# Second block of a two-block network: k, v, q and the Fourier input token major from float32r parts, rotation on the free axis, Fourier over half the tokens

## The chip, the core and the metric

The kernel runs on one core of one Trainium2 chip. A time is device microseconds of one execution; the time of a kernel is the median of several runs.

## What is computed

The reference chains two transformer blocks over 256 tokens of width 1024. The first block (projections, sparse attention, a convolution, a mixture of 64 experts) is not touched by the change. The second block has two layers; the change is in the mixer of its first layer, cut here to what matters:

```python
xn   = modulate(rms_norm_2(h, norm_mix_g), sh1, sc1)      # 256 x 1024
proj = xn @ w_in                                          # Fourier 512, q 512, k 128, v 128
q, k = apply_rope(q, cos, sin), apply_rope(k, cos, sin)   # pairs (2j, 2j+1) of each 64 wide head
attn = window_attention(q, k, v, k_ctx, v_ctx, sink)      # 8 heads, 2 kv heads, 256 + 256 keys
y    = concat([fourier_mix(f_in), attn]) @ w_out
h    = h + g1 * y                                         # then norm, SwiGLU (the first FFN)

def fourier_mix(u):                                       # per head of 128 columns
    return fftn(u, axes=(token, column), norm='ortho').real
```

## The kernel before

The weights stream from HBM through a ring of six slots of 2 MB (`wslot`); SyncE's queue issues the loads in program order, each when its slot is free. In the mixer the slots hold, in order, the k and v columns (`kv2`), q, the Fourier columns (`f`), the two halves of `ada2_2`, the two halves of the output weights (`out2`), `ada2_3`, `ada2_4`, and then the first loads of the FFN, among which are further `ada` matrices.

`even` builds the normalized input (`norm_mod`) feature major, eight tiles of 128 features by 256 tokens, and then weaves four generators: `attention2`, `gemvs2`, `projections`, `second_out`. A model of the engines (`_Model`) decides at build time in which order their instructions are written, and under `manual_schedule` the order so written is the order in which TensorE, VectorE and ScalarE run them. Each engine works its list from the top; nothing behind a waiting instruction starts.

- `projections` computes one 128 column tile after the other (k, q0, v, q1, q2, q3, then four Fourier heads) with float32 matmuls of 256 columns. After k and each q tile, `rope` copies the tile, multiplies it on TensorE by a swap matrix, and combines the two with cosine and sine on VectorE.
- `attention2` works on eight units (four head pairs by two blocks of 128 queries). `scores2` makes a unit's 128x512 scores for two heads and its softmax: VectorE adds the mask and takes the maximum (a custom instruction, printed as CUSTOM_DVE or ISA), ScalarE the exponentials, VectorE and GpSimd scale. `attend2` transposes the probabilities on TensorE, ScalarE copies them (`p2T`), TensorE multiplies with the values. Scores of the next unit are written ahead of the transposes of the present one.
- `dft` makes one Fourier head: two matmuls with the 128 point matrix, a copy (`fz`), four matmuls with the 256 point matrices.
- `gemvs2` makes three gate and scale vectors of the layer on VectorE: eight multiply-adds of 128x1024 each (`acc`), then a sum and a transpose on TensorE. It starts with the event `q1`.
- `second_out` is the output projection: eight tiles of eight matmuls. The first three tiles take the three PSUM banks called `g`; a further tile needs a bank that VectorE has emptied by adding it to `x`.

In the FFN that follows, the weights are used as two float32r parts already: `split2` rounds on ScalarE (`whi`), takes the difference on VectorE or GpSimd (`wlo`), and three matmuls take the place of one. The scheduler, not the written order, places the FFN's first instructions among those of the mixer.

## Time and profile before

| | |
|---|---|
| median of 3 runs | 1718.29 us (1717.68 to 1720.73) |
| profiled execution | 1721.32 us, of which the span of the trace is 1719.5 us |
| busy share of the span | TensorE 79%, VectorE 33%, ScalarE 22%, GpSimd 8% |
| granted TensorE clock, mean | 0.887 |
| DMA | 589.51 MB, mean 343 GB/s |

Shares of the whole span are an average over stages. Until about 1155 us the experts stream their weights and the DMA engines are full; the mixer of the second block lies between about 1164 and 1286 us; after it come the two FFNs with the pooling mixer between them. Times in the text are microseconds from the start of the span.

### The profile page before, as it was taken

To read this page: it belongs to the slowest core of one execution; us is meant where nothing else is said; L and a number is where in the kernel's file an instruction comes from. 1 tells how busy PE (TensorE), PEld (TensorE's weight loads), DVE (VectorE), ACT (ScalarE), POOL (GpSimd) and SP (SyncE) were. 2 spreads that over 40 slices of the span, in tenths; PEclk is the share of its full clock that TensorE was granted. 3 is DMA by queue.
4 is the path that set the end of the run, shared out by engine and by line. 5 is a ranking of instruction groups with operands and counts; after the bars stand their busy time and mean duration, and the time that the engine had idled before them with its cause. 6 is when DMAs were issued, how large, how long until landed. Compare 5 with 4: busy or idle time off the path is not lost.

```text
span 1719.5 us, 18422 instructions
## 1 busy us (share of the span) xinstructions
PE 1361.6 (79%) x7664; PEld 788.7 (46%) x7664; DVE 575.8 (33%) x1109; ACT 375.6 (22%) x704; POOL 143.0 (8%) x80
## 2 busy tenths in 40 slices
PE   7999976666765765666576676769989999999997
PEld 5676832221221221222122212216667778778886
DVE  1577721110110111111011101105575878454533
ACT  2335110000000000100000000013324444554444
POOL 0000000000000000000000000001202232213224
PEclk9999988878887787788788778889999999999999
DMA  9687889999999999899999999997476786635620
GB/s 402 244 342 300 317 370 427 427 426 426 427 428 427 427 426 425 340 427 426 426 426 427 428 427 427 426 426 285 184 298 243 301 340 260 245 147 220 245 74 25
DMA packets 43563, 589.51 MB, mean 343 GB/s; under 512 B 4840, under 2 KB 4968, under 8 KB 6992
## 3 DMA queue, kind: packets, MB, share of 16 engines
q1 hardware_dynamic: 42336, 584.82, 82.2%
q0 software_dynamic: 704, 2.64, 0.4%
q8 instruction: 63, 1.03, 0.2%
q10 hardware_dynamic: 432, 0.79, 0.1%
q14 instruction: 28, 0.23, 0.0%
HBM read 587.16 MB, written 1.06 MB: 342 GB/s over the span
## 4 chain that ended last, share of the span: by engine, by line
PE 31%; DMA 24%; DVE 3%; ACT 1%; issue 0%; DVEq 0%; ACTq 0%
PE ps L264 31%; DMA w<-in_w 22%; DMA w<-in_w2last 1%; DVE acc L264 1%; DMA w<-in_ada 0%; DVE wlo L264 0%; DVE p L264 0%; ACT p L264 0%; DVE x L264 0%; ACT rstd L264 0%; DVE ada L264 0%; DVE sqa L264 0%; DVE mix L264 0%; ACT mix L264 0%; ACT sq L264 0%
## 5 line engine op out<-in xcount | busy, mean ns | idle before, releaser
L264 PE MATMUL ps<-w,xg 128*32 128x512 f32 x2032 | 304.3, 735 | 178.1 <-DMA w<-in_w 177.9
L264 PE MATMUL ps<-w,gT 128*32 128x512 f32 x1024 | 180.7, 843 | 100.3 <-DMA w<-in_w 91.3
L264 PEld LDWEIGHTS ps<-w,xg 128*32 128x32 f32 x2032 | 64.9, 123 | 397.2 <-DMA w<-in_w 208.0
L264 ACT ACTIVATE whi<-w 128x1024 fp32r<-128x1024 f32 x132 | 139.4, 1059 | 152.1 <-PE ps L264 146.5
L264 DVE TENSOR_TENSOR g<-g,ps 128x512 f32<-128x512 f32 x16 | 11.0, 687 | 451.1 <-PE ps L264 451.1
L264 DVE TENSOR_TENSOR wlo<-w,whi 128x1024 fp32r<-128x1024 f32 x88 | 114.6, 1310 | 111.5 <-ACT whi L264 111.5
L264 PE MATMUL ps<-whi,mix 128*128 128x512 f32 x352 | 140.4, 404 | 4.1 <-ACT mix L264 4.1
L264 DVE SCALAR_TENSOR_TENSOR acc<-w,sil,acc 128x1024 f32<-128x1024 f32 x98 | 141.8, 1447 | 2.7 <-DMA w<-in_ada 1.1
L264 POOL TENSOR_TENSOR wlo<-w,whi 128x1024 fp32r<-128x1024 f32 x44 | 112.6, 2569 | 350.2 <-ACT whi L264 293.2
L264 PE MATMUL ps<-wlo,mix 128*128 128x512 f32 x352 | 140.5, 400 | 0.0
L264 PE MATMUL ps<-whi,xl 128*128 128x512 f32 x352 | 138.6, 399 | 0.9 <-DVE xl L264 0.9
L264 PEld LDWEIGHTS ps<-w,gT 128*32 128x32 f32 x1024 | 33.6, 134 | 229.0 <-DMA w<-in_w 147.4
L264 DVE COPY y<-ps 128x512 f32<-128x512 f32 x16 | 11.1, 691 | 282.1 <-PE ps L264 282.1
L264 ACT ACTIVATE gT<-ps 128x512 f32<-128x512 f32 x16 | 9.6, 597 | 320.6 <-PE ps L264 320.6
L264 PE MATMUL ps<-hT,w 128*128 128x256 f32 x320 | 77.4, 389 | 2.4 <-DVE hT L264 2.4
L264 PEld LDWEIGHTS ps<-whi,mix 128*128 128x128 f32 x352 | 67.5, 192 | 22.2 <-ACT mix L264 5.3
L264 DVE SCALAR_TENSOR_TENSOR x<-ps,mod,x 128x256 f32<-128x256 f32 x152 | 67.3, 482 | 28.8 <-PE ps L264 28.6
L264 PE MATMUL ps<-oh,xtok 128*128 128x128 f32 x512 | 62.9, 284 | 16.4 <-DVE oh L264 16.4
L264 PEld LDWEIGHTS ps<-whi,xl 128*128 128x128 f32 x352 | 67.3, 191 | 16.6 <-DVE xl L264 1.7
L264 PEld LDWEIGHTS ps<-wlo,mix 128*128 128x128 f32 x352 | 67.6, 192 | 14.6 <-DVE wlo L264 0.4
L264 PEld LDWEIGHTS ps<-oh,xtok 128*128 128x128 f32 x512 | 61.8, 200 | 18.1 <-DVE oh L264 16.5
L264 PE MATMUL ps<-wlo,gh 128*128 128x512 f32 x176 | 69.7, 399 | 0.0
(302 smaller groups left out, 1511.5 us busy)
## 6 DMA issues: line engine op xcount, KB each, us to landing
w<-in_w SPq DMA_DIRECT2D x190, 2048.0 KB, 26.1
w<-in_ada SPq DMA_DIRECT2D x34, 2048.0 KB, 10.2
w<-in_f SPq DMA_DIRECT2D x32, 2048.0 KB, 8.4
w<-in_wout SPq DMA_DIRECT2D x4, 2048.0 KB, 9.3
w<-in_win SPq DMA_DIRECT2D x3, 2048.0 KB, 23.7
w<-in_conv SPq DMA_DIRECT2D x4, 1536.0 KB, 11.8
w<-in_ada1h SPq DMA_DIRECT2D x2, 2048.0 KB, 13.4
w<-in_cw SPq DMA_DIRECT2D x2, 2048.0 KB, 12.0
```

The costliest lines, as they stand in the source:

```text
L264: r = f(*args, **kw)
```

## The change

The diff, with the constant tables, the packing and some removed lines left out:

```diff
         self.ring = pool("ring", RING)
+        self.xtra = pool("xtra", 4)
...
-    def rope(self, out, ps, scale, name):
...
+    def half(self, w, c):
+        src = w[:, D * c:D * c + D]
+        hi, lo = [self.xtra.tile([P, D], F32R, tag="x", name=self.nm(n)) for n in ("whi", "wlo")]
+        nc.scalar.activation(hi, src, AF.Copy)
+        for eng, s in ((nc.vector, slice(0, 512)), (nc.gpsimd, slice(512, D))):
+            eng.tensor_tensor(lo[:, s], src[:, s], hi[:, s].bitcast(F32), ALU.subtract)
+        return hi, lo
...
+    def tm_gemm(self, ps, chunks, cols):
+        m = D // cols
+        for c in chunks:
+            yield from self.ahead_half(c + 1)
+            ws = self.halves[c]
+            for kk in range(m):
+                k = m * (c - chunks[0]) + kk
+                yield self.ready(ws[1][:, cols * kk:cols * kk + cols], self.hl[:, k, :])
+                for t in range(2):
+                    st = slice(P * t, P * t + P)
+                    hi, lo = [x[:, cols * kk:cols * kk + cols] for x in ws]
+                    self.mm(ps[t][:, :cols], lhsT=self.hh[:, k, st], rhs=hi, start=k == 0, stop=False)
+                    self.mm(ps[t][:, :cols], lhsT=self.hh[:, k, st], rhs=lo, start=False, stop=False)
+                    self.mm(ps[t][:, :cols], lhsT=self.hl[:, k, st], rhs=hi, start=False, stop=k == KT - 1)
+                yield self.clock
+            yield from self.ahead_half(c + 2)
+    def rope(self, src, t, scale):
+        q = self.wk(512, "ada")[:, :n]
+        nc.scalar.activation(q, src, AF.Copy, scale=scale)
...
+        nc.vector.tensor_tensor(pairs(r), pairs(q)[:, :, :, ::-1], sin[:, None].to_broadcast([P, n // 64, 32, 2]), ALU.mult)
...
+        nc.vector.tensor_tensor(qh, qh, cos[:, None].to_broadcast([P, n // 64, 64]), ALU.mult)
+        nc.vector.tensor_tensor(q, q, r, ALU.add)
+        return q
+    def fourier(self, i, f):
         pz = self.ps()
         for t in range(2):
+            self.mm(pz[:, :S], lhsT=f[:, t, P * i:P * i + P], rhs=self.late("dft")[:, S * t:S * t + S],
+                    start=t == 0, stop=t == 1)
+        z = self.ph(S, "fz", 2)
+        nc.scalar.activation(z, pz[:, :S], AF.Copy)
...
+        self.mm(po[:, :129], lhsT=cs[:, :P], rhs=z[:, :129], start=True, stop=True)
+        self.mm(po[:, S:S + 127], lhsT=cs[:, P:], rhs=z[:, 129:], start=True, stop=True)
+        q = self.ph(127, "fq", 2)
+        nc.scalar.activation(q, po[:, S:S + 127], AF.Copy)
+        nc.vector.tensor_copy(o[:, ::P], po[:, :S:P])
+        nc.vector.tensor_tensor(o[:, 1:P], po[:, 1:P], q, ALU.subtract)
+        nc.vector.tensor_tensor(o[:, P + 1:], po[:, P - 1:0:-1], q[:, ::-1], ALU.add)
...
     def projections(self):
+        ps = yield from self.grab("g", 2)
+        yield from self.tm_gemm(ps, (0, 1), S)
+        for t in range(2):
+            nc.vector.tensor_copy(self.vall[:, 0, t, :], ps[t][:, P:S])
+            k.append(self.rope(ps[t][:, :P], t, 1.0))
...
+        yield from self.tm_gemm(ps, (2, 3, 4, 5), 512)
+        q = [self.rope(ps[t], t, 0.125) for t in range(2)]
...
+        self.spawn(self.turned(q, [self.qT[:, :, P * t:P * t + P] for t in range(2)], [f"q{i}" for i in range(4)]))
...
+        yield from self.tm_gemm(ps, (6, 7, 8, 9), 512)
...
+            nc.scalar.activation(f[:, t, :], ps[t], AF.Copy)
...
+    def turned(self, src, outs, names):
...
+                self.tr(pt[:, P * i:P * i + P], x[:, P * i:P * i + P])
+            self.nc.vector.tensor_copy(o, pt[:, :P * n].rearrange("p (i s) -> p i s", i=n))
...
+        self.parts = [("kv2", i) for i in range(2)] + [("q", i) for i in range(4)] + [("f", i) for i in range(4)]
+        self.halves = [self.half(self.ahead[n][0][1], i) for n, i in self.parts[:2]]
+        h = self.hh = self.ph(0, "h", shape=[P, KT, S], dt=F32R)
+        self.hl = self.ph(0, "hl", shape=[P, KT, S], dt=F32R)
...
+        nc.gpsimd.dma_start(self.mask[:, 0, P:2 * P], a["wm"][0])
...
+        self.norm_mod(self.x, self.scaled(self.v2("norm_mix_g_2", 0), self.m2(0, 1)), self.m2(0, 0),
+                      parts=(h, self.hl))
```

The normalized input is now kept as two float32r parts (`hh`, `hl`), and the weights are split in ten pieces of 128x1024 (`half`; two for k and v, four for q, four for the Fourier columns), of which two are in flight. Tokens stand on the output's partitions: k and v are one pass of eight steps of 256 columns, q and the Fourier input one pass each of eight steps of 512 columns. The rotation multiplies by cosine and sine along the free axis; k and q are then turned back by transposes, all four q tiles of 128 tokens together. The Fourier heads transform the tokens first, for 129 of the 256 frequencies, and `mix` gets the other half by mirroring. The constants loaded late shrink from 1088 to 512 KB. Outside the mixer the lists of the engines hold the same instructions in nearly the same order.

Three places show how the lists move. The first is TensorE at the start of attention; `kall` and `qT` are the keys and queries, `rq` a rotated copy, `ada` in the changed kernel holds the rotated q. Before:

```order
L264 MATMUL ps_10304<-h_10223,w_10215 128x256 x8
L264 MATMUL ps_10315<-rq_10313,latet 128x256
L264 MATMUL ps_10321<-h_10223,w_10219 128x256 x8
L264 MATMUL ps_10332<-w_10215,h_10223 128x128 x4
L264 MATMUL ps_10337<-rq_10330,latet 128x256
L264 MATMUL ps_10332<-w_10215,h_10223 128x128 x7
L264 MATMUL ps_10352<-kall,qT_10301 128x512
L264 MATMUL ps_10356<-kall,qT_10301 128x512
```

Now, with the first piece of the Fourier pass (`whi`, `wlo` by `h`, `hl`) ahead of the same first scores:

```order
L260 MATMUL ps_10483<-whi_10465,hl_10237 128x512
L260 MATMUL ps_10490<-firstt,ada_10470 128x128 x4
L260 MATMUL ps_10482<-whi_10465,h_10236 128x512
L260 MATMUL ps_10482<-wlo_10466,h_10236 128x512
L260 MATMUL ps_10482<-whi_10465,hl_10237 128x512
L260 MATMUL ps_10483<-whi_10465,h_10236 128x512
L260 MATMUL ps_10483<-wlo_10466,h_10236 128x512
L260 MATMUL ps_10483<-whi_10465,hl_10237 128x512
L260 MATMUL ps_10502<-firstt,ada_10476 128x128 x4
L260 MATMUL ps_10518<-kall,qT_10322 128x512
L260 MATMUL ps_10522<-kall,qT_10322 128x512
L260 MATMUL ps_10482<-whi_10512,h_10236 128x512
```

The first scores came behind k, q0 and most of v; they now stand behind all of k, v and q, a quarter of the Fourier pass and eight transposes.

The second place is VectorE between the second and the third unit's softmax. Before:

```order
L264 TENSOR_SCALAR p_10368<-p_10368,p2st_10369 128x256 x2
L264 COPY vall<-ps_10332 128x256
L264 TENSOR_TENSOR rt_10430<-ps_10428,latet 128x256
L264 TENSOR_TENSOR rq_10416<-rq_10416,latet 128x256
L264 TENSOR_TENSOR qT_10301<-rq_10416,rt_10430 128x256
L264 TENSOR_SCALAR acc_10436<-w_10284,sil 128x1024
L264 SCALAR_TENSOR_TENSOR acc_10436<-w_10284,sil,acc_10436 128x1024
L264 ISA p_10434,p2st_10435<-ps_10443,mask_10224,nsink_10228 128x512
```

Now:

```order
L260 TENSOR_SCALAR p_10534<-p_10534,p2st_10535 128x256 x2
L260 SCALAR_TENSOR_TENSOR acc_10510<-w_10305,sil,acc_10510 128x1024
L260 SCALAR_TENSOR_TENSOR acc_10510<-w_10307,sil,acc_10510 128x1024 x3
L260 TENSOR_TENSOR wlo_10585<-w_10224,whi_10584 128x512
L260 SCALAR_TENSOR_TENSOR acc_10510<-w_10307,sil,acc_10510 128x1024
L260 ISA p_10598,p2st_10599<-ps_10600,latet,nsink_10241 128x512
```

Two gemv instructions stood there, behind a rotation; now five do, and a half piece of the split, and no other work.

The third place is VectorE where the output projection begins; `x` is the addition that empties a bank, `acc` a gemv (the weights' number tells which load it reads), `wlo` here the split of the FFN's first weights. Before:

```order
L264 SCALAR_TENSOR_TENSOR acc_10671<-w_10294,sil,acc_10671 128x1024 x4
L264 TENSOR_TENSOR mod_90<-ps_10871,vect 128x2x4
L264 TENSOR_SCALAR acc_10875<-w_10296,sil 128x1024
L264 SCALAR_TENSOR_TENSOR acc_10875<-w_10296,sil,acc_10875 128x1024 x3
L264 SCALAR_TENSOR_TENSOR x<-ps_10848,mod_90,x 128x256
L264 SCALAR_TENSOR_TENSOR x<-ps_10849,mod_90,x 128x256
L264 TENSOR_TENSOR sqa_10894<-sqa_10894,sq_10898 128x256
L264 SCALAR_TENSOR_TENSOR x<-ps_10850,mod_90,x 128x256
L264 TENSOR_TENSOR sqa_10894<-sqa_10894,sq_10903 128x256
L264 SCALAR_TENSOR_TENSOR acc_10875<-w_10298,sil,acc_10875 128x1024 x2
```

Now:

```order
L260 SCALAR_TENSOR_TENSOR acc_10922<-w_10319,sil,acc_10922 128x1024 x3
L260 TENSOR_SCALAR acc_11259<-w_11260,sil 128x1024
L260 TENSOR_TENSOR mod_93<-ps_11012,vect 128x2x4
L260 SCALAR_TENSOR_TENSOR acc_11259<-w_11260,sil,acc_11259 128x1024
L260 TENSOR_TENSOR wlo_11161<-w_11154,whi_11160 128x1024
L260 SCALAR_TENSOR_TENSOR mods_11111<-mod_93,vect 128x8
L260 TENSOR_TENSOR wlo_11177<-w_11154,whi_11176 128x1024
L260 SCALAR_TENSOR_TENSOR acc_11259<-w_11260,sil,acc_11259 128x1024
L260 TENSOR_TENSOR wlo_11193<-w_11154,whi_11192 128x1024
L260 TENSOR_TENSOR wlo_11209<-w_11154,whi_11208 128x1024
L260 SCALAR_TENSOR_TENSOR x<-ps_10988,mod_93,x 128x256
L260 SCALAR_TENSOR_TENSOR x<-ps_10989,mod_93,x 128x256
```

Before, the first additions to `x` came ahead of the second half of the layer's last gemv (`w_10298`) and of the FFN's split. Now that gemv is through when they come, and they stand behind three instructions of the FFN's own gemv (`w_11260`) and all four pieces of the FFN's split.

## Rows read from the trace of the kernel before

**Rows 1.** Busy time by stage: us, each engine's busy us (instructions), granted clock, DMA share, GB/s
```profile
1180.30:1252.80 72.50, 66.78 (x407) 48.08 (x408) 44.98 (x105) 25.28 (x67) 18.72 (x16) 0.98 0.47 178
1252.80:1283.00 30.20, 29.88 (x149) 24.57 (x147) 25.22 (x33) 7.26 (x13) 0.00 (x0) 1.00 0.81 311
1283.00:1292.60 9.60, 3.28 (x7) 1.68 (x7) 5.64 (x11) 3.03 (x7) 0.00 (x0) 0.67 0.93 372
1292.60:1310.00 17.40, 17.40 (x69) 14.05 (x69) 13.45 (x21) 8.29 (x12) 0.00 (x0) 0.89 0.69 278
```

**Rows 2.** TensorE in order of time: start, us, instructions merged; idle before, releaser
```profile
1252.78 3.19 PE L264 MATMUL ps<-mix,w 128*128 128x256 f32 x14
...
1257.85 15.27 PE L264 MATMUL ps<-mix,w 128*128 128x256 f32 x70
...
1275.03 7.93 PE L264 MATMUL ps<-mix,w 128*128 128x256 f32 x36
```

**Rows 3.** VectorE in order of time: norm, softmax of units 1, 4 and 5, one gemv
```profile
1165.13 3.25 DVE L264 SCALAR_TENSOR_TENSOR nt<-x,mods,rstd 128x256 f32<-128x256 f32 x8 [2.18 <-ACT rstd L264]
...
1180.34 0.75 DVE L264 CUSTOM_DVE_ANT_0 p<-ps,mask,nsink 128x512 f32<-128x512 f32 x1 [1.51 <-PE ps L264]
...
1201.05 0.74 DVE L264 CUSTOM_DVE_ANT_0 p<-ps,mask,nsink 128x512 f32<-128x512 f32 x1
...
1204.64 1.27 DVE L264 SCALAR_TENSOR_TENSOR acc<-w,sil,acc 128x1024 f32<-128x1024 f32 x1
...
1208.16 0.75 DVE L264 CUSTOM_DVE_ANT_0 p<-ps,mask,nsink 128x512 f32<-128x512 f32 x1
```

**Rows 4.** TensorE groups of the mixer, 1164 to 1284: count, busy us, mean ns
```profile
L264 PE MATMUL ps<-h,w 128*128 128x256 f32 x144 | 36.8, 399 | 2.1 <-ACT h L264 2.1
...
L264 PE MATMUL ps<-w,h 128*128 128x128 f32 x32 | 4.4, 281 | 0.0
...
L264 PE MATMUL ps<-rq,latet 128*128 128x256 f32 x10 | 3.2, 401 | 0.5 <-ACT rq L264 0.5
...
L264 PE MATMUL ps<-latet,ff 128*128 128x256 f32 x16 | 4.5, 405 | 0.5 <-ACT ff L264 0.5
...
L264 PE MATMUL ps<-latet,fz 128*128 128x256 f32 x32 | 8.0, 391 | 0.8 <-DVE fz L264 0.8
```

**Rows 5.** TensorE inside one attention unit, in order of time
```profile
1205.87 1.09 PE L264 MATMUL ps<-p2T,vall 128*64 128x128 f32 x16
...
1206.89 1.13 PE L264 MATMUL ps<-kall,qT 64*128 64x512 f32 x4
```

**Rows 6.** Busy time in 10 us of the first FFN, columns as in rows 1
```profile
1300.00:1310.00 10.00, 10.00 (x46) 8.07 (x44) 6.05 (x9) 5.24 (x8) 0.00 (x0) 1.00 0.57 211
```

**Rows 7.** VectorE groups, 1164 to 1287: count, busy us, mean ns, idle before
```profile
L264 DVE SCALAR_TENSOR_TENSOR acc<-w,sil,acc 128x1024 f32<-128x1024 f32 x24 | 30.7, 1280 | 0.4
...
L264 DVE TENSOR_SCALAR acc<-w,sil 128x1024 f32<-128x1024 f32 x4 | 3.0, 748 | 0.5 <-PE ps L264 0.5
...
L264 DVE COPY fz<-ps 128x512 f32<-128x512 f32 x4 | 2.7, 684 | 5.6 <-PE ps L264 5.6
```

**Rows 8.** ScalarE group of the hi parts, 1164 to 1320
```profile
L264 ACT ACTIVATE whi<-w 128x1024 fp32r<-128x1024 f32 x13 | 13.4, 1057 | 6.5 <-PE ps L264 4.8 <-issue 1.7
```

**Rows 9.** VectorE, first additions to x in the output projection
```profile
1263.67 0.92 DVE L264 SCALAR_TENSOR_TENSOR x<-ps,mod,x 128x256 f32<-128x256 f32 x2 [0.82 <-PE ps L264]
```

**Rows 10.** An ada load: issue on SyncE's queue, then KB and us to landing
```profile
1262.88 0.33 SPq L453 DMA_DIRECT2D w<-in_ada  x1
...
w<-in_ada SPq DMA_DIRECT2D x1, 2048.0 KB, 8.4
```

**Rows 11.** Busy time and granted clock before, between and after two pauses of TensorE
```profile
1166.80:1170.20 3.40, 3.40 (x10) 2.69 (x9) 1.59 (x5) 2.15 (x6) 0.00 (x0) 0.50 1.04 440
1224.60:1227.00 2.40, 0.00 (x0) 0.00 (x0) 1.49 (x8) 2.10 (x7) 0.00 (x0) 1.00 0.00 0
1228.20:1231.60 3.40, 3.40 (x21) 2.33 (x19) 2.59 (x4) 0.20 (x1) 1.56 (x1) 0.51 0.00 0
```

More of the change, by code (lines that the diff above doesn't have):

```diff
@@ L109, in _rope @@
     ang = np.concatenate([row[:, None] * inv[None], col[:, None] * inv[None]], axis=-1)
-    a = np.repeat(ang.T, 2, axis=0)
-    a = np.concatenate([a, a], axis=0)
-    swap = np.zeros((P, P), np.float32)
-    i = np.arange(0, P, 2)
-    swap[i + 1, i] = -1.0
-    swap[i, i + 1] = 1.0
-    return np.cos(a).astype(np.float32), np.sin(a).astype(np.float32), swap
+    a = np.repeat(ang, 2, axis=1)
+    sign = np.where(np.arange(64) % 2 == 0, -1.0, 1.0).astype(np.float32)
+    tm = lambda x: x.astype(np.float32).reshape(2, P, 64).transpose(1, 0, 2)
+    return tm(np.cos(a)), tm(np.sin(a) * sign)
 def _dft():
@@ L156, in _consts @@
     l = _Pack()
-    cos, sin, swap = _rope()
-    l.add("swap", swap)
+    cos, sin = _rope()
     l.add("cos", cos)
     l.add("sin", sin)
-    cs, c256, s256 = _dft()
+    cs, f = _dft()
     l.add("cs128", cs)
-    l.add("c256", c256)
-    l.add("s256", s256)
-    i, j = np.arange(P)[:, None], np.arange(P)[None]
-    l.add("wm0", np.where(j <= i, 0.0, NEG))
-    l.add("wm1", np.where(j >= i, 0.0, NEG))
+    l.add("dft", f)
     return c, l
@@ L1641, in fourier @@
-    def fourier(self, i):
-        nc = self.nc
-        w = yield from self.take("f")
-        ps = yield from self.grab()
-        yield from self.fgemm_steps(ps[:, :S], w[:, i, :], self.hT)
-        f = self.ph(S, "ff", 2)
-        nc.scalar.activation(f, ps[:, :S], AF.Copy)
-        self.release(ps)
-        self.spawn(self.dft(i, f))
-    def dft(self, i, f):
+        src = w[:, D * c:D * c + D]
+        hi, lo = [self.xtra.tile([P, D], F32R, tag="x", name=self.nm(n)) for n in ("whi", "wlo")]
@@ new lines, in half, with ahead_half @@
+        nc.scalar.activation(hi, src, AF.Copy)
+        for eng, s in ((nc.vector, slice(0, 512)), (nc.gpsimd, slice(512, D))):
+            eng.tensor_tensor(lo[:, s], src[:, s], hi[:, s].bitcast(F32), ALU.subtract)
+        return hi, lo
+    def ahead_half(self, n):
+        while len(self.halves) < min(n, len(self.parts)):
+            name, c = self.parts[len(self.halves)]
+            w = yield from self.take(name)
+            self.halves.append(self.half(w, c))
+    def tm_gemm(self, ps, chunks, cols):
[14 more added lines that the diff above has]
+            yield from self.ahead_half(c + 2)
@@ L1754, in projections @@
-        self.done("q")
-        for i in range(4):
-            yield from self.fourier(i)
-        self.done("f")
-        self.events["projections"] = True
+        ps = yield from self.grab("g", 2)
+        yield from self.tm_gemm(ps, (0, 1), S)
+        k = []
+        for t in range(2):
+            nc.vector.tensor_copy(self.vall[:, 0, t, :], ps[t][:, P:S])
+            k.append(self.rope(ps[t][:, :P], t, 1.0))
+        self.release(*ps)
+        self.done("kv2")
+        self.events["v"] = True
@@ new lines, in projections @@
+        self.spawn(self.turned(k, [self.kall[:, 0, None, P * t:P * t + P] for t in range(2)], ["k"]))
+        ps = yield from self.grab("g", 2)
+        yield from self.tm_gemm(ps, (2, 3, 4, 5), 512)
+        q = [self.rope(ps[t], t, 0.125) for t in range(2)]
+        self.release(*ps)
+        self.done("q")
+        self.spawn(self.turned(q, [self.qT[:, :, P * t:P * t + P] for t in range(2)], [f"q{i}" for i in range(4)]))
+        ps = yield from self.grab("g", 2)
+        yield from self.tm_gemm(ps, (6, 7, 8, 9), 512)
@@ new lines, in projections @@
+        f = self.ff
+        for t in range(2):
+            nc.scalar.activation(f[:, t, :], ps[t], AF.Copy)
+        self.release(*ps)
+        self.done("f")
+        yield self.ready(f)
+        for i in range(4):
+            yield from self.fourier(i, f)
+        self.events["projections"] = True
+    def turned(self, src, outs, names):
+        for x, o in zip(src, outs):
+            yield self.ready(x)
+            yield self.room("n")
+            pt = self.ps("n")
+            n = o.shape[1]
+            for i in range(n):
+                self.tr(pt[:, P * i:P * i + P], x[:, P * i:P * i + P])
+            self.nc.vector.tensor_copy(o, pt[:, :P * n].rearrange("p (i s) -> p i s", i=n))
+        for n in names:
+            self.events[n] = True
```

80 lines of the change are left out of this document (26 added, 54 removed).

## Prediction

> **What bounds the kernel now.** I read the windows by stage first: they show the mixer as two stretches. From the first softmax (1180.3) to the output projection (1252.8) TensorE is busy 66.8 of 72.5 us, VectorE 45.0, ScalarE 25.3, GpSimd 18.7; in the output projection (30.2 us) TensorE is busy 29.9 [rows 1]. So TensorE is the nearest bound here, the transfers are not (178 GB/s in the first stretch), and the FFN that follows keeps TensorE at 17.4 of 17.4 [rows 1]: whatever delays its start delays the end by as much. Then the order of time: when attention starts (1180.34), how long a unit of it takes (1201.05 to 1208.16, 7.1) [rows 3], when the projection starts (1252.78) and ends (1275.03 + 7.93 = 1282.96) [rows 2]. The bound by TensorE holds only as long as its list has other work between the steps of a unit; in a unit VectorE alone needs 1201.05 to 1204.64, 3.6 us, and after it come copies, transposes, values and scores in series.
>
> **What TensorE saves.** A float32 matmul leaves two records; 70 records in 15.27 us are 0.218 each, 0.43 a matmul of 256 columns [rows 2]. A float32r matmul of 512 columns takes 0.22 to 0.23 (46 in 10 us, two of them transposes) [rows 6]; three replace one float32 product. Removed: 144 records of h, 32 of half width for v (0.11), 10 of the swap, 48 of the Fourier stage [rows 4]: 31.4 + 3.5 + 2.2 + 10.5 = 47.6. Added: 96 float32r matmuls of 512 columns (22.1), 48 of 256, ten transposes (1.2), eight float32 matmuls of 256 columns (3.5) and four pairs of 129 and 127 (1.7). For 256 columns no row exists: between half the 512 price, 0.11, and that price, 0.23; I take 0.12, since the half width float32 record costs half, so 5.8. The Trainium skill, "TensorE: Matmul & The Clock Gate", section "Wait — 56ns, not 53.3ns?", states columns over 2.4 GHz plus 2.5 ns, 109 ns here, which would make the term 5.2. Sum added 34.3, saved about 13 us.
>
> **Where attention now starts.** Norm: VectorE makes 16 pieces instead of 8, at 3.25/8 = 0.41 [rows 3], so the last `hl` comes at 1165.2 + 6.5 = 1171.7. The eight k and v steps follow those pieces; TensorE runs the first ones at the low clock, as it does now in 1166.8 to 1170.2 (0.50) [rows 11], which makes k and v complete at about 1174.4. The first two weight splits lie in the pauses of the experts' tail, the third behind the norm; each needs 1.06 on ScalarE [rows 8] and half a VectorE piece, 0.6. q: 48 x 0.23 = 11.1, plus 1.1 because the fourth split's VectorE half stands behind the rotation of k, ends at 1186.6. Rotation of q on VectorE: six passes of 128x512 at 0.65 (the 512 wide copy takes 0.684 [rows 7]; 0.5 to 0.75 as bounds), then two copies, one short gemv (0.75), a split half (0.6), one gemv (1.2) before the first softmax: about 1194.3. That is 14.0 later than now. Bounds: 11.5 if the low clock and the 1.1 fall away, 19 if 256 columns cost 0.23.
>
> **How long the units take.** With TensorE's filling work cut, the lists of VectorE and the series inside a unit set the pace. Unit 1 to 2: 3.6 + one gemv 1.2 = 4.8. Unit 2 to 3: 3.6 + five gemvs at 1.28 [rows 7] + a split half 0.6 = 10.5; TensorE waits there too, since the gemv's sum stands in its list ahead of the next Fourier piece. Units 3 to 8: softmax and its exponentials 2.3 until ScalarE copies the previous unit's transposes, copy and transposes to 4.2, then half a Fourier piece (1.4, part hidden), values 1.05 and scores 1.1 [rows 5]: five times 7.1, as now. Last unit to projection: 9.1 (its softmax 3.6, transposes, copies and values of two units 2.9, Fourier matmuls between them 2.6). Sum 59.9 against 72.4 now, so the projection starts at 1254.2, 1.4 later than 1252.78. The 13 us saved are eaten by 14 of later start.
>
> **The output projection.** TensorE stops twice. Its list holds the gemv's sum after ten matmuls (4.3 us), while VectorE ends that gemv 5.6 after the start: 1.3. Then the fourth tile needs a bank. `x` stands on VectorE behind three instructions of the FFN's first gemv and four splits at 1.2. That gemv's weights are asked for when the slot of the layer's last gemv's first half is free, 0.4 before the projection starts, and land 8.4 later [rows 10], at 8.0; three gemvs and four splits make 8.0 more, so `x` comes at 16.0 and its bank at 16.5, where TensorE ended its third tile at 12.55: 4.0. Now, `x` waits for TensorE and not the other way (idle 0.82 [rows 9]). Against that, the 30.2 us now hold 64 matmuls at 0.43 and two gemv sums (2.6 together), of which one moves ahead of the stretch (-1.3), and VectorE has one gemv instruction less behind the last tile (-1.3 [rows 7]). Sum +2.7.
>
> **The start of the FFN.** 3.28 of 9.6 us busy before 1292.6, and a clock of 0.89 after it [rows 1]; VectorE's list there loses four gemvs, now done earlier. TensorE is already gapless after 1292.6, so the gain is no more than the waits before: 1.2 (0 to 3.4).
>
> **The clock.** After a pause of 2.4 us TensorE ran 3.4 us at 0.51 [rows 11]: 1.7 us lost. The new lists make such pauses at units 2 to 3 (5.9), 3 to 4 and 5 to 6 (2.4 each) and in the projection (4.0). All on the path would be 6.8, none 0; I take 3.5.
>
> Edits at no cost: the Fourier copies move to ScalarE (25.3 of 72.5 busy), masks come by their own transfers on GpSimd during the experts, the shorter constants leave the queue 1.3 us earlier; all wait for nobody now. Uncovered, a Fourier head's tail would cost about 1 us.
>
> **Sum.** +1.4 +2.7 -1.2 +3.5 = +6.4 on the span of 1719.5, so 1725.9; the execution's own time 1721.3 becomes 1727.7. The median of the runs shown stands 3.0 below that execution: 1718.3 + 6.4 = 1724.7.
>
> **Rivals.**
> *TensorE is the bound after all.* If VectorE keeps ahead, the 13 us leave the path: 1705.6. For it: 66.8 of 72.5 busy. Against: the unit pace of 7.1 already holds where VectorE is busy between softmaxes, and the start moves by 14. It decides if the first softmax comes before about 1188. Part of it (half) gives 1712.
> *A draw.* The pauses don't lower the clock, and `x` comes some us earlier because the splits run in VectorE's pauses: +2 or less, 1719.5.
> *The clock stays low through attention.* TensorE is busy about 5.9 of 7.1 us a unit at full rate; at half rate its share in a unit's series (values, scores, transposes, about 2.7) doubles: +2.7 in three of six units, 8 more than forecast, 1732.7. For it: both pauses shown did it. Against: after each the full clock was back within 3.5 us. The Trainium skill, same page, section "A second HAM failure mode: psum-queue depth-cycling", describes matmul groups with small idle gaps between them as making the clock swing and costing throughput. By that rule this rival holds; the trace agrees for the two pauses, not for the gaps under 1 us around them, which ran at 1.00.
>
> **How the numbers follow.** Forecast 0.46, draw 0.27, TensorE bound in full or half 0.18, low clock 0.09. The predicted time is the forecast's, 1724.7; its own range is 1720 to 1730. Leaving out the full saving and the worst of the low clock, the range is 1711 to 1731. A difference under 0.2% (3.4 us) is about what measuring this kernel can't tell from none. Faster by more 0.18, within 0.28 (the draw and the forecast's lower edge), slower 0.54.
>
> **What would show it.** In the changed kernel's trace: first softmax at about 1194; unit 2 to 3 about 10.5 apart with TensorE waiting for `acc`; projection starting near 1254 to 1258; TensorE idle about 4 us before the fourth tile, released by `x`; granted clock near 0.5 behind these pauses. The prediction is wrong if the rotation takes VectorE half as long, if units run at under 6 us, or if `x` comes before the third tile ends.

## The result, and the profile after

The changed kernel takes 1729.0 us (median of 5 runs, 1728.7 to 1733.1) where the kernel before takes 1718.3 (5 runs, 1717.7 to 1720.7): ratio 1.0065, 95% interval 1.0054 to 1.0077. It is slower by 10.7 us; I had forecast 6.4 slower, in a range of 1711 to 1731. The profiled execution took 1728.9, its span is 1727.0.

Single executions differ by some us in the experts' stage, which the change does not touch: in the 14 traces of this study the wait of 2.07 or 2.08 us that opens the norm (TensorE's first wait for `h`) ends between 1164.8 and 1170.0, with no pattern by kernel. So I compare stretches counted from the end of that wait: to the first softmax, and to the FFN's second product (the first matmul with `gh`, the gated hidden values). From there to the end all traces take 400.5 to 403.6 us.

Behind that wait traces differ by chance too. Up to the output projection e6 and e7 below have the same lists on TensorE and VectorE, yet e7 starts the projection 4.0 us earlier, counted from the norm's wait; the granted clock over 1200 to 1210 was 0.50 in e6 and 0.77 in e7. The changed kernel and e2 have the same lists there as well, and e2 is 2.1 us later. So a stretch of a single trace holds some 4 us of chance, and where it disagrees with the ratio of the medians, the ratio counts.

| from the end of the norm's wait, us | before | after | difference |
|---|---|---|---|
| first softmax | 14.1 | 30.5 | +16.4 |
| last softmax | 68.5 | 84.8 | +16.3 |
| output projection starts | 86.6 | 94.6 | +8.0 |
| output projection ends | 116.8 | 129.0 | +12.3 |
| FFN's second product | 150.0 | 157.6 | +7.6 |

The stretch is 7.6 us longer, the medians differ by 10.7. The 3 us between them are those by which the profiled execution of before lay above its own median; which stage of it was long, two traces can't say.

Windows by stage of the changed kernel: norm to first softmax, to the projection, projection, start of the FFN, the 10 us after it, then four short stretches behind waits of TensorE. Columns as in [rows 1].

```profile
1164.24:1196.80 32.56, 26.20 (x129) 20.31 (x128) 22.70 (x42) 12.41 (x20) 9.95 (x6) 0.95 0.84 352
...
1196.80:1260.90 64.10, 47.76 (x304) 30.41 (x302) 49.10 (x111) 26.95 (x70) 24.25 (x18) 0.89 0.44 165
1260.90:1295.33 34.43, 30.86 (x139) 25.60 (x138) 24.09 (x32) 7.06 (x12) 0.00 (x0) 0.95 0.78 305
1295.33:1303.07 7.74, 4.04 (x12) 2.94 (x11) 5.35 (x14) 4.03 (x9) 0.00 (x0) 0.80 0.96 381
1303.07:1313.00 9.93, 9.93 (x44) 8.11 (x43) 6.00 (x10) 6.09 (x9) 0.00 (x0) 0.98 0.29 125
1201.00:1203.50 2.50, 2.50 (x8) 1.85 (x7) 2.17 (x6) 1.13 (x3) 1.45 (x1) 0.50 0.00 0
1214.20:1217.80 3.60, 3.60 (x14) 2.87 (x11) 1.65 (x7) 2.05 (x7) 1.73 (x2) 0.50 0.96 332
1225.00:1228.60 3.60, 3.47 (x22) 2.55 (x22) 3.60 (x5) 1.39 (x2) 3.60 (x3) 0.54 0.00 0
1276.16:1280.00 3.84, 3.84 (x10) 3.16 (x11) 2.69 (x5) 1.21 (x3) 0.00 (x0) 0.56 0.85 290
```

Against [rows 1] TensorE's busy time between first softmax and projection fell from 66.8 to 47.8 us, but the stretch only from 72.5 to 64.1, and the mean clock from 0.98 to 0.89: at half rate even the work that is left takes longer. In the projection TensorE now waits (30.9 of 34.4 busy), where it did not.

VectorE in order of time: the last `hl` of the norm, the pass of the rotation that took longest, the second transposed copy of q, softmax of units 1 and 2, the gate vector's products, softmax of unit 3.

```profile
1171.44 0.49 DVE L260 SCALAR_TENSOR_TENSOR hl<-nt,mod,h 128x256 fp32r<-128x256 f32 x1 [0.18 <-ACT h L260]
...
1188.55 0.69 DVE L260 TENSOR_TENSOR ada<-ada,rt 128x512 f32<-128x512 f32 x1
1189.35 1.58 DVE L260 TENSOR_TENSOR rt<-ada,latet 128x512 f32<-128x512 f32 x1
...
1193.73 0.69 DVE L260 COPY qT<-ps 128x512 f32<-128x512 f32 x1 [0.75 <-PE ps L260]
...
1196.80 0.75 DVE L260 CUSTOM_DVE_ANT_0 p<-ps,latet,nsink 128x512 f32<-128x512 f32 x1
...
1201.59 0.74 DVE L260 CUSTOM_DVE_ANT_0 p<-ps,latet,nsink 128x512 f32<-128x512 f32 x1
...
1205.17 6.22 DVE L260 SCALAR_TENSOR_TENSOR acc<-w,sil,acc 128x1024 f32<-128x1024 f32 x4
...
1213.10 0.75 DVE L260 CUSTOM_DVE_ANT_0 p<-ps,latet,nsink 128x512 f32<-128x512 f32 x1
```

These answer to [rows 3]: the norm ends where forecast, attention starts at 1196.8 instead of 1180.3, and between units 2 and 3 stand four products in one row. TensorE in order of time, its main waits and the projection, answers to [rows 2]:

```profile
1193.04 0.66 PE L260 MATMUL ps<-firstt,ada 128*128 128x128 f32 x4 [1.62 <-DVE qT L260]
...
1213.23 1.08 PE L260 MATMUL ps<-acc,cont 128*32 128x256 f32 x8 [4.65 <-DVE acc L260]
...
1260.90 4.58 PE L260 MATMUL ps<-mix,w 128*128 128x256 f32 x20
...
1276.16 19.17 PE L260 MATMUL ps<-mix,w 128*128 128x256 f32 x80 [3.21 <-DVE x L260]
...
1296.97 0.67 PE L260 MATMUL ps<-sqa,firstt 128*128 128x256 f32 x2 [1.64 <-DVE sqa L260]
```

The wait for `acc` and the wait for `x` stand where the prediction put them. The 80 records behind the second take 0.240 each instead of 0.218, which is 1.7 us of low clock.

### The profile page after: what moved, and what is told of

The parts are those of the page before. It is cut to its first block, busy times and chain, and to the rows that moved or that the text cites. A ratio compares the mean times of both kernels' runs of the same rounds, so it can differ in the third digit from the quotient of the medians.

```text
span 1727.0 us, 18396 instructions
## 1 busy us (share of the span) xinstructions
PE 1347.4 (78%) x7616; PEld 779.2 (45%) x7616; DVE 591.2 (34%) x1137; ACT 386.3 (22%) x715; POOL 162.0 (9%) x90
## 3 DMA queue, kind: packets, MB, share of 16 engines
q8 instruction: 62, 1.02, 0.2%
## 4 chain that ended last, share of the span: by engine, by line
PE 31%; DMA 23%; DVE 4%; ACT 2%; issue 1%; DVEq 0%; ACTq 0%
PE ps L260 31%; DMA w<-in_w 23%; DVE acc L260 1%; ACT p L260 0%; DVE wlo L260 0%; DVE p L260 0%; DVE x L260 0%; DVE ada L260 0%; ACT p2T L260 0%; ACT rstd L260 0%; DVE mix L260 0%; DVE sqa L260 0%; ACT whi L260 0%; DVE nt L260 0%; DVE rt L260 0%
## 5 line engine op out<-in xcount | busy, mean ns | idle before, releaser
L260 PE MATMUL ps<-w,xg 128*32 128x512 f32 x2032 | 299.9, 726 | 177.2 <-DMA w<-in_w 177.1
L260 ACT ACTIVATE whi<-w 128x1024 fp32r<-128x1024 f32 x142 | 149.9, 1058 | 156.9 <-PE ps L260 153.0
L260 POOL TENSOR_TENSOR wlo<-w,whi 128x1024 fp32r<-128x1024 f32 (+1 forms) x54 | 129.1, 2402 | 409.5 <-ACT whi L260 349.9
L260 DVE TENSOR_TENSOR wlo<-w,whi 128x1024 fp32r<-128x1024 f32 (+1 forms) x98 | 123.5, 1268 | 122.4 <-ACT whi L260 122.3
## 6 DMA issues: line engine op xcount, KB each, us to landing
w<-in_conv SPq DMA_DIRECT2D x4, 1536.0 KB, 11.5
```

Source lines behind the costliest of these rows:

```text
L260: r = f(*args, **kw)
```

## The experiments

Theory A is the prediction's: the end moves with the path, a later start goes through, and each wait in the lists costs what it takes. The rivals: what is gained at one wait is waited for at the next (B); the planner, which has one price for all matmuls, writes the lists wrongly (C); the low clock carries the loss. All ratios are to the kernel before, with their 95% intervals; the two columns behind them are us of one trace each, from the end of the norm's wait.

| run | ratio | first softmax | to FFN's second product |
|---|---|---|---|
| before | 1 | 14.1 | 150.0 |
| after | 1.0065 (1.0054 to 1.0077) | 30.5 | 157.6 |
| e1 no rotation of q | 1.0054 (1.0041 to 1.0066) | 27.6 | 157.5 |
| e2 x first | 1.0053 (1.0040 to 1.0066) | 30.2 | 156.9 |
| e3 products late | 1.0081 (1.0068 to 1.0094) | 28.4 | 160.6 |
| e4 planner's price | 1.0006 (0.9997 to 1.0015) | 29.9 | 146.7 |
| e5 q in halves | 1.0157 (1.0144 to 1.0170) | 20.9 | 171.8 |
| e6 halves and price | 1.0029 (1.0018 to 1.0040) | 24.0 | 153.7 |
| e7 halves, price, x first | 1.0024 (1.0012 to 1.0035) | 22.9 | 150.2 |
| e8 Fourier part alone | 0.9963 (0.9950 to 0.9976) | 14.1 | 142.4 |
| e9 q and k by tile | 1.0094 (1.0078 to 1.0109) | 21.6 | 163.3 |
| e10 by tile, x first | 1.0070 (1.0056 to 1.0083) | 21.5 | 159.6 |
| e11 TensorE kept busy | 1.0050 (1.0037 to 1.0064) | 30.3 | 156.1 |
| e12 Fourier part alone, x first | 0.9952 (0.9935 to 0.9969) | 12.4 | 141.2 |

**e1, does a later start go through?** The planner is still charged for the three passes of each of q's two blocks of tokens, but they are not written.

```diff
+        if n > P:
+            for o, i in ((r, q), (q, q), (q, r)):
+                self.model.issue("vector", "tensor_tensor", (o, q, i, ALU.add), {})
+            return q
```

> The changed kernel without the six VectorE passes that rotate q (q is copied and transposed unrotated; the output is therefore not the reference's); the order of all other mixer work is the same. Theory A (the later start of attention goes through to the end, because the units after it are a chain whose pace does not depend on when it starts): six passes at 0.72 plus the 0.9 that one of them lost are gone, the first softmax comes at about 1191.7 instead of 1196.8, and the end is 4 to 5.5 us earlier than in the changed kernel: 1724 us, ratio to the kernel before 1.003 to 1.004. Rival B (what is gained at the start is waited for again later, at the gate and scale vectors or at the weights): first softmax 5 earlier, but the end less than 1.5 us earlier, ratio 1.0055 to 1.0065.

The first softmax came 2.9 us earlier, not 5: with the passes gone the second transposes stand behind six Fourier steps in TensorE's list. The end moved by 0.1 us in the stretch and 0.3 by the medians; the ratios differ by 1.9 us, but their intervals overlap. Both halves of theory A's number failed, but B's reason (a wait at the products) does not show either: the gap between units 2 and 3 stayed 11.5. In this trace the gain was lost behind TensorE's two waits of 2.49 us, ahead of units 5 and 7: what follows ran at half rate both times, in the changed kernel only the first time. TensorE behind the first:

```profile
1221.67 2.78 PE L260 MATMUL ps<-p2T,vall 128*64 128x128 f32 x16
...
1224.38 2.08 PE L260 MATMUL ps<-kall,qT 64*128 64x512 f32 x4
```

At full rate these take 1.09 and 1.13 [rows 5]. The cycles of units 4 to 5 and 6 to 7 were 8.9 and 8.4 us, 7.8 and 6.8 in the changed kernel: 2.7 us given back. That this follows from the earlier start is not shown: e2, which starts no earlier, ran at half rate in the same two places. Without it most of the 2.9 would have reached the end, so e1 leaves theory A's main point open.

**e2, the wait for x.** Each split's low part on VectorE and each gate vector's first product in the FFN gets a dependency that only orders, on the third addition to `x`.

```diff
+        if t == 2:
+            self.third = d
...
+        if eng is self.nc.vector:
+            self.after_third(d)
...
+                    if not slots and hasattr(self, "sqx"):
+                        self.after_third(d)
```

> The changed kernel, but VectorE's splits and vector products of the FFN are ordered behind the third addition to x. Theory A: TensorE's pause of 3.2 us before the fourth output tile goes, and with it the low clock behind it (80 records at 0.240 instead of 0.218, 1.7 us): the norm of the FFN comes 4 to 5 us earlier than in the changed kernel; the end 3 to 5 us earlier, 1724 to 1726 us, ratio 1.0035 to 1.005. Rival B (the splits and products that were done in the projection are now late for the FFN): TensorE waits at the start of the FFN for the lo parts by what it no longer waits in the projection, ratio 1.006 to 1.007.

The wait and the low clock behind it are gone: the projection took 29.3 us instead of 34.4. TensorE from the fourth tile to the norm:

```profile
1271.87 22.61 PE L260 MATMUL ps<-mix,w 128*128 128x256 f32 x104
1297.77 1.09 PE L260 MATMUL ps<-sqa,firstt 128*128 128x256 f32 x2 [3.29 <-DVE sqa L260]
```

But the whole stretch is only 0.7 shorter: 2.1 were lost before the projection (again two units at half rate, 8.9 and 8.4 us), where the lists are those of the changed kernel, so that loss is chance. And the wait for `sqa` grew from 1.64 to 3.29, since the products and splits moved there; one product on VectorE waits there 1.90 us for its weights. The local price of the wait is confirmed (5.1 for 4.9 expected). As a gain it is about 1 us by the medians and 2 by the ratios, between theory A and rival B, and the intervals of e2 and the changed kernel overlap.

**e3, the products moved out of the gap.** The event `s2` is set behind the third unit's scores.

```diff
+                    self.events[f"s{n}"] = True
...
     def gemvs2(self):
-        yield self.event("q1")
+        yield self.event("s2")
```

> The changed kernel, but the vector products of the layer start after the third unit's scores instead of when q is there. Theory A: the 11.5 us between the second and third softmax become about 6 to 7.5, the low clock after TensorE's wait of 4.65 goes, and the output projection starts 4 to 6 us earlier; the products end up to 5 us later in it, so the end is 2 to 5 us earlier than in the changed kernel: ratio 1.0035 to 1.0055. Rival B (VectorE's total in this stage is the bound: 46.5 of 61.5 us busy, plus what it waits in the chain): the products removed from that place delay the projection or x by the same amount, ratio 1.006 to 1.007 or above.

The gap fell to 6.5 and the projection started 6.7 us earlier, a little more than theory A says. Then rival B collected: TensorE in the projection and before the norm,

```profile
1270.52 0.64 PE L260 MATMUL ps<-acc,cont 128*32 128x256 f32 x8 [1.63 <-DVE acc L260]
...
1278.70 0.69 PE L260 MATMUL ps<-firstt,ada 128*128 128x128 f32 x2 [4.76 <-ACT ada L260]
...
1300.83 1.19 PE L260 MATMUL ps<-sqa,firstt 128*128 128x256 f32 x2 [4.58 <-DVE sqa L260]
```

waits for what VectorE had put off. The kernel is 3.6 us slower than the changed one by the medians, though the ratios' intervals overlap. Neither of the two orders is free: in one heap the products held up a unit, put off they held up the projection and the FFN.

**e4, the planner's price.** The build-time model charges 1.67 ns a column for every matmul. That is float32 (256 columns in 0.43); 512 float32r columns take 0.23, and it believes 0.86.

```diff
-            n = int(np.prod(ins[-1].shape[1:])) * 1.67e-3 if op == "matmul" else 0.11
+            n = int(np.prod(ins[-1].shape[1:])) * (0.45e-3 if ins[-1].dtype == F32R else 1.67e-3) if op == "matmul" else 0.11
```

> The changed kernel with one number of the build-time model altered: it holds 1.67 ns a column for every matmul, so it takes a float32r matmul of 512 columns for 0.86 us where the trace shows 0.23; now 0.45 ns a column for float32r. The instructions are the same, their order differs. Theory C (the wait between the second and third unit is a planner's mistake: it believes that a pair of 512 column steps covers four vector products): with the right price the four products in one row are spread, the 11.5 us become 6 to 8, and the end is 3 to 8 us earlier than in the changed kernel: ratio 1.002 to 1.005. Rival A2 (the order hardly matters, the series inside a unit and VectorE's total set the pace): within 1.5 us of the changed kernel, ratio 1.0055 to 1.0075.

The same instructions in another order are 8.7 us faster by the medians and 10.9 by the traces, with the first softmax nearly as late as without the edit (29.9). By its ratio e4 can't be told from the kernel before. Theory C's direction holds, and its amounts do not: the gap of 11.5 became 9.9 and not 6 to 8, so the four products were only part of it, and the gain is above the 3 to 8 us expected. TensorE around the last units:

```profile
1250.28 2.32 PE L260 MATMUL ps<-mix,w 128*128 128x256 f32 x10
1253.36 0.65 PE L260 MATMUL ps<-firstt,p 128*128 128x128 f32 x4 [0.76 <-ACT p2T L260]
...
1260.60 5.88 PE L260 MATMUL ps<-mix,w 128*128 128x256 f32 x26
1268.23 4.15 PE L260 MATMUL ps<-mix,w 128*128 128x256 f32 x18 [1.76 <-DVE x L260]
```

The planner now knows that the Fourier columns are soon done, finishes the Fourier heads between earlier units, and fills the last units with the projection's first matmuls: these begin 0.15 us before the last softmax, where in the changed kernel they begin 9.8 behind the last. From last softmax to the end of the projection it takes 36.3 us, in the changed kernel 44.3; from first to last softmax it takes 50.5 instead of 54.3. The clock has a part in it. Windows from first softmax to the end of the projection, of the changed kernel, then of e4:

```profile
1196.80:1295.33 98.53, 78.61 (x442) 56.01 (x440) 73.18 (x142) 34.01 (x82) 24.25 (x18) 0.91 0.56 214
```

```profile
1199.90:1286.75 86.85, 71.70 (x440) 51.71 (x440) 69.27 (x138) 34.12 (x82) 25.61 (x18) 0.96 0.55 210
```

The stretch is 11.7 us shorter, and TensorE is busy 6.9 us less with the same work, at 0.96 instead of 0.91. That the order is worth 8.7 us rests on the medians; how much of it comes through fewer waits and how much through the clock that follows them, the traces don't separate.

**e5 to e7, an earlier start.** q in two halves of 256 columns, the first rotated while TensorE makes the second; then with the price of e4; then also with the order of e2.

```diff
-        yield from self.tm_gemm(ps, (2, 3, 4, 5), 512)
-        q = [self.rope(ps[t], t, 0.125) for t in range(2)]
...
+        for h in range(2):
+            ps = yield from self.grab("g", 2)
+            yield from self.tm_gemm(ps, (2 + 2 * h, 3 + 2 * h), S)
+            q = [self.rope(ps[t][:, :S], t, 0.125) for t in range(2)]
...
```

> The changed kernel, but q is made in two halves of 256 columns (two heads pairs each, both blocks of tokens), and the first half is rotated and transposed while TensorE makes the second; the planner keeps its price of 1.67 ns a column for float32r. The first softmax should come at about 1186.5 (k and v 1174, half of q 5.5, the wait 1.1, six passes of 256 columns at about 0.4 and transposes), 10 earlier than in the changed kernel. Theory A (start goes through to the end): 7 to 10 us earlier, ratio 0.9995 to 1.0025. Theory C (the order made from the wrong price sets the end, the start is only lost again): at most 3 us earlier, ratio 1.0045 to 1.0065.

> Both edits: q in two halves, and the planner's price of a float32r column at 0.45 ns. Theory A (start counts in full once the order is right): 7 to 10 us below the run with the price alone (1.0006), ratio 0.9945 to 0.9965. Theory C (start is absorbed): within 2 us of it, ratio 0.9995 to 1.0015. In between, 3 to 6 us, if the second half of q and the Fourier columns now make TensorE the bound between the units: ratio 0.997 to 0.999.

> As the run with halves and price, and VectorE's FFN splits and products ordered behind the third addition to x. Where x still stands behind splits in that run, TensorE's pause before the fourth output tile (1.8 to 3.2 us) goes: 1 to 4 us less than that run. If the splits are then late at the start of the FFN, 0 to 1 us more than that run.

The start came 9.6 us earlier in e5 and the kernel was 15.5 us slower than the changed one: outside both theories. VectorE's list shows where most of it went; the second half's rotation and six products stand between units 4 and 5, and two passes of the rotation took 1.52 and 1.37 us instead of 0.42 beside a split on GpSimd:

```profile
1214.77 1.52 DVE L261 TENSOR_TENSOR rt<-ada,latet 128x256 f32<-128x256 f32 x1
1216.32 1.37 DVE L261 TENSOR_TENSOR ada<-ada,latet 128x256 f32<-128x256 f32 x1
...
1226.63 0.74 DVE L261 CUSTOM_DVE_ANT_0 p<-ps,latet,nsink 128x512 f32<-128x512 f32 x1
```

20.9 us pass between those softmaxes. With the right price (e6) most of that is gone, but a start 6 us earlier than e4's did not make the kernel faster: by the medians e6 is 3.3 us slower than e4, outside all three cases expected. Its trace ends 7.0 later, in part by chance. Scores of an early unit, in e6 and then in e7, whose lists are the same up to the projection:

```profile
1207.86 2.07 PE L261 MATMUL ps<-kall,qT 64*128 64x512 f32 x2
```

```profile
1206.21 1.12 PE L261 MATMUL ps<-kall,qT 64*128 64x512 f32 x2
```

Of the 3.5 us that e7 is shorter, 4.0 arose ahead of its edit; from the projection's start on it took 62.0 us, e6 61.5. By the medians x first is worth 0.9, and the intervals overlap. So an earlier start alone gained nothing here. In e5 the passes and products between the softmaxes ate it; in e6 the low clock takes part, and the two are not separated.

**e8 and e12, the Fourier part alone.** The kernel before with its k, v, q and rotation, the Fourier columns token major in float32, and the half-token Fourier of the change; e12 adds e2's ordering.

```diff
-        for i in range(4):
-            yield from self.fourier(i)
...
+                self.mm(ps[t], lhsT=self.at(self.hT, k)[:, P * t:P * t + P], rhs=w[:, 512 * k:512 * k + 512],
+                        start=k == 0, stop=k == KT - 1)
...
+        for i in range(4):
+            yield from self.fourier(i, f)
```

> The kernel before with the Fourier part of the change alone: k, v, q feature major in float32 with the rotation on TensorE as before; the Fourier columns token major in float32 (the same TensorE time, 13.8 us), then the half-token Fourier. TensorE saves about 5.3 us of 66.8 in the stage, all else starts when it did. If TensorE's work is the bound of the stage: 4 to 5.3 us faster than before, ratio 0.997 to 0.9975. If the chain inside the units is (theory A): 0 to 2 us faster, ratio 0.999 to 1.000. If the Fourier heads, which now wait for all their columns, come too late for the projection: slower by up to 4 us, ratio up to 1.0025.

> The kernel before with the Fourier part alone, and VectorE's FFN splits and products ordered behind the third addition to x. The pause before the fourth output tile is 1.0 us there; if it goes and nothing is late for the FFN: about 1 us less than the Fourier part alone, ratio 0.9955 to 0.996; if the FFN's splits come later for it: 0.9965 to 0.9975.

e8 beats both kernels: 1712.4 against 1719.3 in the same rounds. Windows from first softmax to the end of the projection, first of the kernel before, then of e8:

```profile
1180.34:1282.97 102.63, 96.62 (x554) 72.62 (x553) 70.17 (x137) 32.53 (x80) 18.72 (x16) 0.98 0.57 217
```

```profile
1182.46:1279.45 96.99, 91.19 (x506) 62.44 (x505) 71.48 (x147) 33.58 (x83) 18.72 (x16) 0.98 0.62 236
```

TensorE loses 5.4 busy us and the stretch 5.6: in the kernel before TensorE is the bound, and theory A's case for this run (0 to 2) falls. e12 measured 1711.6, not to be told from e8. Its edit did not reach what it was meant for: the pause of 1.02 us before the fourth tile stays, since `x` stands there behind the layer's own products. The first softmax, 1.7 earlier with the same lists, is chance.

**e9 and e10, an attempt at both.** Float32r parts and the new Fourier, but k and q tile by tile, feature major, with the swap on TensorE, and e4's price; e10 adds e2's ordering.

```diff
+            self.mm(ps, lhsT=hi[:, s], rhs=self.hh[:, k, :], start=k == 0, stop=False)
+            self.mm(ps, lhsT=lo[:, s], rhs=self.hh[:, k, :], start=False, stop=False)
+            self.mm(ps, lhsT=hi[:, s], rhs=self.hl[:, k, :], start=False, stop=k == KT - 1)
```

> The changed kernel's Fourier part and float32r parts kept, but k and q made tile by tile and feature major (three float32r matmuls of 256 columns in the place of one float32, 24 x 0.114 = 2.7 us a tile instead of 3.4), v token major, the rotation on TensorE by the swap matrix as in the kernel before, the planner's price of a float32r column at 0.45 ns; to make room, two instead of three buffers for the probabilities and one for a Fourier copy. So attention starts after k, v and one tile of q: first softmax about 17 us after the wait that opens the norm (14.1 in the kernel before, 30.5 in the changed kernel, 29.9 with the price alone). If the early start and TensorE's saving both count (TensorE was the bound of the stage, as the Fourier part alone showed): the stage from first softmax to projection takes 52 to 60 us against 72.4 in the kernel before and 64.9 with the Fourier part alone, and the kernel is 9 to 18 us faster than before, ratio 0.9895 to 0.995. If VectorE's products and softmaxes set the pace as soon as TensorE has less to do: no better than the Fourier part alone, ratio 0.9955 to 0.9985.

> As the run by tile, and VectorE's FFN splits and products ordered behind the third addition to x. Where the run by tile has x behind splits, as the changed kernel does (TensorE waits 3.2 us there), 1 to 4 us less than the run by tile; if the splits come late for the FFN, or the order there was right already, within 1 us of it.

Neither came near what was expected: e9 is slower than the changed kernel, e10 not to be told from it. The first softmax came at 21.6, not 17: v in 128 column matmuls took 6.0 us for 48, hardly less each than 256 columns, and the first tile of q ran mostly at half rate, behind a wait of 0.95. Windows of v and of that tile:

```profile
1172.80:1178.80 6.00, 6.00 (x51) 5.95 (x51) 1.35 (x3) 1.33 (x2) 1.28 (x1) 0.95 1.01 426
1178.80:1183.60 4.80, 3.85 (x20) 3.66 (x20) 1.72 (x3) 1.06 (x1) 1.78 (x1) 0.65 1.00 427
```

Units 3 to 7 then took 8.9 to 9.9 us each, with splits and rotations of later tiles between the softmaxes on VectorE. The run changed several things at once, so it does not say which of these weighs most. The ordering of e10 shortened the projection from 37.8 to 34.3 us and gained 5.3 by the medians.

**e11, the clock.** Eight matmuls that nobody reads, in three of TensorE's waits; everything else in the same order.

```diff
+            if g and fill:
+                self.busy(self.psp.tile([P, 512], F32, tag="psn", name=self.nm("ps"), bufs=1), fill)
...
+        if slots == "ada2_2":
+            self.busy(ps, 4)
```

> The changed kernel with eight float32 matmuls of 512 columns added whose results nobody reads, placed in three of TensorE's waits: four (3.4 us) before the first gate vector's sum, in the wait of 4.65, and two (1.7 us) before the second transposes in each of the two waits of 2.49; all other orders are the same. If the low clock behind these waits is what I charged 3.5 us for: the matmuls behind them run at full rate (a pair of 512 column steps at 0.23 and not 0.43, values 1.09 and not 2.64), the stage from first softmax to projection falls from 64.1 us by 2 to 4, ratio 1.004 to 1.0055. If the clock behind a wait does not depend on such work, or its cost lies off the path: no change, ratio 1.006 to 1.007; if the added matmuls themselves hold up the list, up to 1.0085.

TensorE at the longest wait, then windows behind the first two filled waits and of the whole stage:

```profile
1208.10 3.60 PE L1733 MATMUL ps<-x 128*128 128x512 f32 x8
1212.90 0.64 PE L260 MATMUL ps<-acc,cont 128*32 128x256 f32 x8 [1.21 <-DVE acc L260]
```

```profile
1213.80:1217.40 3.60, 3.03 (x17) 2.27 (x16) 2.50 (x9) 2.72 (x8) 1.66 (x2) 1.00 1.03 337
1223.20:1226.80 3.60, 3.19 (x25) 1.85 (x26) 3.60 (x5) 1.32 (x2) 3.60 (x3) 1.00 0.00 0
1196.47:1258.03 61.56, 51.30 (x320) 30.60 (x318) 49.00 (x111) 26.84 (x70) 24.81 (x18) 0.97 0.45 172
```

The clock is 1.00 where it was 0.50 and 0.54, and the stage takes 61.6 us instead of 64.1: more work on TensorE, 2.5 us less time in this trace. At the FFN's second product 1.5 of it are left. The ratio fell by 0.0015, but the intervals overlap, so the end's gain is not shown. In the changed kernel's trace only two of the three filled waits were followed by a low clock.

## Why the prediction was right, and where its reasons were not

**What TensorE saves: confirmed.** A float32r matmul of 256 columns stands 0.113 to 0.114 apart in the k and v steps at full rate, 0.213 at half; I had taken 0.12. k and v were complete at 1174.0 (1174.4), q at 1186.7 (1186.6).

**Where attention starts: too short by 2.5.** +16.5, not +14.0. The steps were those named. The missing time is 0.9 for one pass of 1.58 instead of 0.65 beside a GpSimd split, some 0.4 for passes 0.72 apart, some 0.4 for ScalarE's copy of q ahead of the first pass, and the 0.75 that VectorE waits for the second transposes, which wait themselves for the bank that the first copy of q still reads.

**How long the units take: place right, reason incomplete.** 64.1 us from first softmax to projection against 59.9 and the part of the 3.5 us of low clock that falls there. Units 1 to 2 took 4.8 (4.8), 2 to 3 11.5 (10.5), the five others 38.0 (35.5), the last to the projection 9.8 (9.1). The wait for `acc` came, 4.65 us. But I read that row of products from the written order and took it for a property of the kernel. e4 shows that most of the loss comes from the order, and the order from one price: by the medians that number alone accounts for 8.7 of the 10.7 us. The forecast's "five times 7.1, as now" had also taken one pair of units [rows 3] for all: the five cycles between units 3 and 8 took 38.0 in the changed kernel, 7.6 each.

**The 13 us saved, eaten by the 14 of later start: right as a sum, not shown as a cause.** e5 and e6 start 6 to 10 us earlier and are not faster than the changed kernel and e4, from which they differ in that start. What e8 shows is the other side: where the start stays, a TensorE saving of 5.4 comes through in full. All else in the change (k, v and q token major, and the float32r parts of their weights and of the Fourier columns') costs the difference between e8 and the changed kernel, about 17 us by the medians, of which e4 gives 8.7 back. The rest is not split further: e5 to e7 move the start only together with VectorE's list, and in e1 the clock hid what came of it.

**The output projection: +2.7, measured +4.2.** The stop at the fourth tile, released by `x`, took 3.21 (4.0), and the first stop 0.37 (1.3); the 1.7 of low clock behind the fourth tile's stop stood in the clock's term. e2 prices stop and clock at 5.1 together.

**The start of the FFN: -1.2, measured -4.7.** From the end of the projection to the FFN's second product it takes 28.6 us instead of 33.3. 1.7 of it are the shorter wait for `sqa`, and a wait of 0.94 for `xl` is gone. Most of the rest is the clock: in the kernel before TensorE ran at half rate from 1289.6 to 1296.5, in the changed one only from 1299.7 to 1303.1, and behind 1303 it ran at 0.98. My bound for this term was 3.4; it counted waits alone, though [rows 1] show 0.67 and 0.89 for the clock there. In another trace this part may come out otherwise.

**The clock: 3.5.** 2.5 by e11 in the units and 1.7 in the projection make 4.2. This was the term with the weakest ground. It is about right for this trace; in e1 and e2 the units took 2.5 us longer by the clock behind the same waits.

**The rivals.** "TensorE is the bound after all" is true of the kernel before and of e8, and false of the changed kernel, whose TensorE waits 16 of the 64 us. "The clock stays low through attention" came only in part: the mean over the stage is 0.89. In the Trainium skill, "TensorE: Matmul & The Clock Gate", section "A second HAM failure mode: psum-queue depth-cycling", small gaps between groups of matmuls make the clock swing. The traces agree in places: behind waits of 0.44, 0.73 and 0.29 us the clock was 0.50 from 1201.0 to 1203.5, and in e9 it was 0.65 behind one of 0.95; behind waits of 1.15 to 1.28 in e11 it stayed at 1.00.

The sum of the terms came to +6.4, the traces differ by 7.5 in span, the medians by 10.7. Errors of both signs (+2.5 at the start, +0.7 in the units once the clock's 3.5 is counted there, +1.5 in the projection, -3.5 in the FFN) leave about +1.2 in the traces, so part of the closeness is luck. The other 3 us between 7.6 and 10.7 are the profiled execution of before, 3.0 above its median; I had carried the same difference over to the median.

## What to carry to other kernels

When a cheaper instruction enters a kernel whose order comes from a cost model, change the model's price with it: here that one number gave back 8.7 of the 10.7 us that the change had lost. Split a change before judging it: one part (Fourier, 7 us faster) was good, and the other hid it. Work saved on the engine that bounds a stage shortens the time only as long as the other engines' lists don't then hold it up; this is argued from e8, where the saving came through, against the changed kernel, where it did not. And judge by the medians of many executions: the same list took up to 4 us more or less in single traces, with the clock that it happened to get.

## What the runs showed of the hardware that I had not expected

A GpSimd instruction that had started first slowed VectorE. GpSimd in the changed kernel:

```profile
1188.79 1.59 POOL L260 TENSOR_TENSOR wlo<-w,whi 128x512 fp32r<-128x512 f32 x1 [1.68 <-ACT whi L260]
```

The VectorE pass at 1189.35, which begins while this split runs, took 1.58; the one ahead of it, of the same size and begun before the split, 0.69. The Trainium skill, "SBUF — State Buffer", section "Who interferes with whom", says that a VectorE instruction with two inputs in SBUF contends with a GpSimd instruction that reads SBUF, and that the ports they share are an exclusive lock, so that the order of issue decides which of them is held up. The trace agrees within 0.14 us: the rest of the split, 1.03, and 0.69 are 1.72.

A float32r matmul of 128 columns is hardly cheaper than one of 256: 0.111 apart in e9 against 0.113 to 0.114. And the same wait of 2.49 us at the same place of the list was followed by half rate in e1 and e2 and by full rate in the changed kernel (values 1.09 at 1241.56, ahead of unit 7), so the cost of a wait of that size in one trace is not its cost in the next.
